# Forgetting attention in a two-layer decoder trunk: the gates' running sums added to the scores on VectorE from a table that is broadcast through memory, instead of by a product with a selection matrix

## The chip, the cores and the metric

The kernel runs on one core of one Trainium2 chip. The core has five instruction streams that run side by side and each in its own order: TensorE (PE in the profile, its weight loads are PEld), VectorE (DVE), ScalarE (ACT), GpSimd (POOL) and SyncE (SP), which here issues all DMA transfers. The metric is the device time of one execution in microseconds (us), as the median of several executions. The activations and the weights are float32; large products are made from float32 values that are split in a high and a low part.

## The reference, cut to what matters

The trunk has two layers over 256 tokens of 1024 values. Layer 0 mixes tokens with forgetting attention ("FoX", 16 heads of 64), layer 1 with latent attention. Each layer has two SwiGLU half-steps and an embedding gate around its mixer. Only the mixer of layer 0 is touched:

```
def fox_mixer(x, w_in, b_f, w_o):
    h = x @ w_in
    q = h[..., :D_MODEL].reshape(B, S, FOX_HEADS, FOX_HEAD_DIM)
    k = h[..., D_MODEL:2 * D_MODEL].reshape(B, S, FOX_HEADS, FOX_HEAD_DIM)
    v = h[..., 2 * D_MODEL:3 * D_MODEL].reshape(B, S, FOX_HEADS, FOX_HEAD_DIM)
    f_logit = h[..., 3 * D_MODEL:].astype(jnp.float32) + b_f.astype(jnp.float32)
    cum = jnp.cumsum(jax.nn.log_sigmoid(f_logit), axis=1).transpose(0, 2, 1)
    ...
        s = jnp.einsum('bqhd,bkhd->bhqk', qb, k).astype(jnp.float32) * scale
        return s + cb[:, :, :, None] - cum[:, :, None, :]
    ...
    o = causal_block_attention(scores, v)
    return o.reshape(B, S, D_MODEL) @ w_o
```

`qb` and `cb` are the queries and their running sums; the last call does the causal mask, the softmax and the product with v. `cum[h, t]` is the running sum of the log gates of head h up to token t. The term of the query is constant along a row of the scores; the term of the key, `-cum[h, s]`, differs from column to column and is what the change moves to another engine.

## The kernel before

**Precision.** A float32 operand is split in hi (ScalarE copies it to fp32r) and lo (VectorE subtracts hi); a product is hi·hi + hi·lo + lo·hi, three matmuls (`mm3`). Weights come from memory in `raw` tiles of 1 MB (three buffers), are split by L193/L194 (or L201/L205, the two halves apart) into `hl` slots and then used. `Stream` plans where in the program each split stands, by estimated clocks of PE, ACT and DVE that `busy()` advances; `load()` issues the next `raw` transfer on SP as soon as a group of weights is split, so SP waits there for the DVE instruction that frees the buffer.

**FoX, before the heads.** `fox()` first makes V (`VA`, `VB`, `VC`). `VC` also yields the 16 gate logits of each token. `gates()` transposes them (so that head h sits in partition 112+h, time along the free dimension) and puts the rest of the gate's work in small steps s1 to s6 into the queue `bg`, one of which is taken out at each `use` of a weight and at k = 3 and 6 inside `ws`. The steps compute log sigmoid (ACT Exp and Ln, some POOL arithmetic at L931 to L941, one DVE reciprocal), the running sum over time (a scan on DVE, L946, into `sc`), and `m8` = -8 times it (POOL, L947). Steps s4 to s6 lay `m8`, split in hi and lo, into `negc` [128, 384]: ACT L951 and L952, DVE L955, L958 and L962. `sel` [128, 16] is a constant 0/1 matrix that picks a head.

**The heads.** Eight rounds j = 0 to 7, two heads each (s = 0, 1, in partitions 0 to 63 and 64 to 127 of the `qk` tile). In round j PE makes k of the next pair (`gen_k(j+1)`, 24 matmuls), the transposes of the finished probabilities of the last pair (`T(j-1)`), the scores (`QK(j)`), q of the next pair (`gen_q(j+1)`, 24 matmuls) and the product with V (`AV(j-1)`). In round 7 the output projection `O` takes the place of the generators. `QK(j)` first fills each of the two score banks with one product of 64 contraction rows and 384 columns, the selection column of the head times `negc`, which puts -8·cum of every key in every row; the 12 matmuls of q·k are accumulated on top. Of the 384 columns, 0:128 are query block 0 against keys 0 to 127, and 128:384 are query block 1 against all 256 keys.

`softmax(j)` runs on DVE and ACT: L1028 adds the causal mask `self.mask` to the bank, scales it by -1/8 and takes the row minimum, four times; L1035 and L1036 do a small correction of that minimum with `cq`, the running sums by token (cum of the query drops out of the softmax); ACT L1040 takes the exponential, four times. `divide` is one DVE reciprocal and two POOL multiplications (L1050) for each head. `T(j)` in the next round needs what L1050 wrote.

**The tile `gb`** holds gain and bias of a layer norm (L543, L544: two broadcast transfers of 512 KB). In FoX it is loaded for the norm after the mixer, in round 2.

What sets the order around the change: each engine runs its list in order, so an instruction that waits holds up everything behind it on its engine; SP's list has the weight transfers and the small ones in one line.

## Time and profile before

| | us |
|---|---|
| median of three runs (lowest, highest) | 1077.59 (1077.35, 1078.14) |
| the profiled execution, whole | 1080.02 |
| its span in the profile | 1077.9 |
| busy in the span: PE, PEld | 1064.3, 974.0 |
| busy in the span: DVE, ACT, POOL | 721.5, 543.8, 60.2 |
| one matmul of `negc` with `sel` (16 of them, in eight pairs) | 0.44 |
| first and last pair start at | 222.0, 280.5 |

The profile shows one execution. All times below are microseconds from the start of its span. "Busy" of PE is modelled, since matmuls overlap: where one ends is less certain than where it starts, so distances between starts are the safer measure. A row of the timeline gives start, duration, engine, line, operation, tiles written and read, shapes and, in brackets, how long the engine sat idle before it and what ended that. A row with "x12" is twelve instructions in a line, and its duration runs from the first start to the last end. The rounds of FoX lie between 222 and 289 us.

### The profile page before, as it was taken

The page shows a single profiled execution, that of the slowest core. Times are in us where ns is not written, and L with a number is a line of the kernel's source. Part 1 is how long each engine was busy: PE and PEld are TensorE (multiplying, and loading weights), DVE is VectorE, ACT ScalarE, POOL GpSimd, SP SyncE. Part 2 cuts the span into 40 slices and gives each one's busy share as a digit, 9 for nine tenths or more (in the row PEclk, how much of TensorE's full clock was granted, in tenths as well). Part 3 has the DMA queues.
Part 4 walks back from the last instruction along what each step waited for, and adds up shares of the span by engine and source line. Part 5 has one row for each costly group of instructions (what it writes and reads, how often), then busy time and mean ns, then how long its engine had stood idle before and what let it go on. Part 6 is the DMA issues. An engine that isn't in the chain of part 4 may idle for free.

```text
span 1077.9 us, 17528 instructions
## 1 busy us (share of the span) xinstructions
PE 1064.3 (99%) x7236; PEld 974.0 (90%) x7236; DVE 721.5 (67%) x1053; ACT 543.8 (50%) x805; POOL 60.2 (6%) x94
## 2 busy tenths in 40 slices
PE   9999999999999999999999999999999999999997
PEld 8989998999889899998899999988889789898986
DVE  5675545788897545548966554389877886455566
ACT  5654433667655444444564443337666465344431
POOL 0000000223100000001320000010000000000000
PEclk9999999999999999999999999999999999999999
DMA  7885642543348655444477554334334568555502
GB/s 276 335 297 222 236 159 93 204 173 118 130 177 296 233 191 196 146 177 166 168 262 274 195 194 148 108 93 147 130 126 159 185 225 314 181 207 188 186 11 78
DMA packets 33092, 199.58 MB, mean 185 GB/s; under 512 B 3699, under 2 KB 5491, under 8 KB 12149
## 3 DMA queue, kind: packets, MB, share of 16 engines
q1 hardware_dynamic: 33012, 198.47, 51.5%
q8 instruction: 57, 0.93, 0.3%
q14 instruction: 23, 0.18, 0.1%
HBM read 197.40 MB, written 1.05 MB: 184 GB/s over the span
## 4 chain that ended last, share of the span: by engine, by line
PE 87%; DVE 8%; ACT 2%; issue 1%; POOL 1%; DMA 0%; DVEq 0%; SPq 0%; POOLq 0%; ACTq 0%
PE y L489 31%; PE h L489 31%; PE tr L489 22%; DVE hl L194 2%; PE tr L493 2%; ACT P L1425 1%; DVE x L569 1%; ACT hl L193 1%; DVE PT L499 1%; DVE tr L1420 0%; DVE st L551 0%; DVE x L550 0%; PE h L493 0%; DVE qk L499 0%; DVE hl L205 0%
## 5 line engine op out<-in xcount | busy, mean ns | idle before, releaser
L194 DVE TENSOR_TENSOR hl<-raw,hl 128x1024 fp32r<-128x1024 f32 (+3 forms) x267 | 312.8, 1191 | 149.5 <-ACT hl L193 148.3
L193 ACT ACTIVATE hl<-raw 128x1024 fp32r<-128x1024 f32 (+3 forms) x267 | 269.3, 1031 | 184.9 <-PE y L489 97.6
L489 PE MATMUL y<-hl,g 128*128 128x512 f32 x816 | 190.7, 390 | 0.0
L489 PE MATMUL h<-xT,hl 128*128 128x256 f32 x1560 | 188.0, 280 | 0.4 <-DVE hl L233 0.2
L489 PEld LDWEIGHTS h<-xT,hl 128*128 128x128 f32 x1560 | 183.4, 190 | 2.6 <-ACT xT L498 0.6
L489 PEld LDWEIGHTS y<-hl,g 128*128 128x128 f32 x816 | 152.0, 188 | 30.7
L489 PE MATMUL tr<-xT,hl 128*128 128x256 f32 x1512 | 176.6, 277 | 0.0
L489 PEld LDWEIGHTS tr<-xT,hl 128*128 128x128 f32 x1512 | 174.2, 188 | 0.5
L489 PE MATMUL h<-hl,xT 128*128 128x512 f32 (+2 forms) x300 | 67.8, 374 | 0.4 <-DVE xT L499 0.4
L489 PE MATMUL y<-hl,xT 128*128 128x512 f32 (+3 forms) x360 | 65.4, 334 | 0.0
L489 PEld LDWEIGHTS h<-hl,xT 128*128 128x128 f32 x300 | 53.2, 188 | 10.7 <-DVE xT L499 1.0
L489 PEld LDWEIGHTS y<-hl,xT 128*128 128x128 f32 x360 | 55.5, 188 | 6.3 <-ACT xT L498 0.4
L561 POOL TENSOR_TENSOR rs<-ve,mhalf 128x1 f32<-128x1 f32 x16 | 15.1, 943 | 633.7 <-DVE ve L560 633.7
L489 PE MATMUL y<-hl,otb 128*128 128x512 f32 x168 | 43.8, 402 | 1.2 <-DVE otb L499 1.0
L499 DVE TENSOR_TENSOR g<-P,g 128x512 fp32r<-128x512 f32 x38 | 26.3, 693 | 26.6 <-ACT g L498 26.6
L498 ACT ACTIVATE xT<-tr 128x512 fp32r<-128x512 f32 x28 | 16.1, 597 | 49.3 <-PE tr L493 49.3
L498 ACT ACTIVATE g<-P 128x512 fp32r<-128x512 f32 x38 | 24.1, 634 | 32.7 <-DVE P L678 32.7
L489 PEld LDWEIGHTS y<-hl,otb 128*128 128x128 f32 x168 | 30.6, 192 | 7.8 <-DVE otb L499 1.4
L194 DVE TENSOR_TENSOR otb<-raw,otb 128x1024 fp32r<-128x1024 f32 (+1 forms) x20 | 24.1, 1203 | 17.3 <-ACT otb L193 17.3
L194 DVE TENSOR_TENSOR qk<-raw,qk 128x1024 fp32r<-128x1024 f32 (+1 forms) x21 | 25.7, 1222 | 12.0 <-ACT qk L193 12.0
L677 ACT ACTIVATE P<-tr 128x512 f32<-128x512 f32 x20 | 12.0, 600 | 39.3 <-PE tr L489 39.3
L678 DVE TENSOR_TENSOR P<-P,tr 128x512 f32<-128x512 f32 x20 | 13.8, 688 | 25.0 <-PE tr L489 13.4
(264 smaller groups left out, 1411.1 us busy)
## 6 DMA issues: line engine op xcount, KB each, us to landing
raw<-in_ffn_in_dram SPq DMA_DIRECT2D x85, 1024.0 KB, 4.9
raw<-in_ffn_out_dram SPq DMA_DIRECT2D x44, 1024.0 KB, 5.0
raw<-in_pg_dram SPq DMA_DIRECT2D x8, 1024.0 KB, 4.8
raw<-in_mo_dram SPq DMA_DIRECT2D x8, 1024.0 KB, 4.7
raw<-in_kq_dram SPq DMA_DIRECT2D x8, 640.0 KB, 5.2
gb<-in_ln_g_dram SPq DMA_DIRECT2D x8, 512.0 KB, 5.8
gb<-in_ln_b_dram SPq DMA_DIRECT2D x8, 512.0 KB, 7.3
raw<-in_fk_dram SPq DMA_DIRECT2D x4, 1024.0 KB, 4.9
```

The source lines that it names most:

```text
L193: nc.scalar.activation(hi, src, AF.Copy)
L194: nc.vector.tensor_tensor(lo, src, hi.bitcast(F32), op=ALU.subtract)
L489: self.nc.tensor.matmul(out, lhsT, rhs, start=start, stop=stop)
L493: self.nc.tensor.transpose(out, in_, self.ident)
L498: self.nc.scalar.activation(hi, src, AF.Copy)
L499: self.nc.vector.tensor_tensor(lo, src, hi.bitcast(F32), op=ALU.subtract)
L561: nc.gpsimd.tensor_tensor(rs, ve, self.mhalf, op=ALU.pow)
L569: nc.vector.scalar_tensor_tensor(xs, xs, rs if i else mv[:, 0:1], self.gb[:, i, c0:c1], op0=ALU.mult if i else ALU.subtract, op1=ALU.add i ...
L677: nc.scalar.activation(gt, ps[0], AF.Silu)
L678: nc.vector.tensor_tensor(gt, gt, ps[1], op=ALU.mult)
L1425: nc.scalar.activation(P[:, c0:c1], b[:, c0:c1], AF.Exp, bias=nm[:, q : q + 1], scale=-1.0, accum_out=su[:, q : q + 1],)
```

## The change

The table of -8·cum now goes out to memory and comes back broadcast: step s4 stores the 16 rows of `m8` in a DRAM tile `fox_c` [16, 256]; `decay_load(j)` reads the two rows of round j back into all 128 partitions of a new tile `mb` [128, 2, 2, 384] (two buffers by j modulo 2, two heads, 384 columns), in two transfers, columns 0:128 and 128:384; `decay_mask(j)` writes the causal mask's -1e30 into it with two POOL instructions (L928), one for each diagonal block. `softmax` reads `mb` where it read `self.mask`, so the same DVE instruction now adds mask and decay. `sel`, `negc`, steps s5 and s6 and the product in `QK` go. In the gate's steps, two subtractions move from POOL to DVE and an idle step goes. `mb` takes the memory of `gb`; so the load of the layer norm's gain and bias moves from round 2 to the end of round 7's softmax.

```diff
-        sel = self.tl([128, 16], F32R, "sel", 1)
-        negc = self.tl([128, 384], F32R, "negc", 1)
+        mb = self.tl([128, 2, 2, 384], F32, "gb", 1)
...
+        def decay_load(j):
+            if not self.rec:
+                o = mb[:, j % 2]
+                for c0, n in ((0, 128), (128, 256)):
+                    row = self.fox_c[2 * j, 0:1]
+                    src = bass.AP(tensor=row.tensor, offset=row.offset, ap=[[0, 128], [256, 2], [1, n]])
+                    nc.sync.dma_start(o[:, :, c0 : c0 + n], src)
+        def decay_mask(j):
+            for c0 in (0, 256):
+                o = mb[:, j % 2, :, c0 : c0 + 128]
+                nc.gpsimd.affine_select(
+                    out=o, in_=o, pattern=[[0, 2], [-1, 128]], compare_op=ALU.is_ge, fill=NEG,
+                    base=0, channel_multiplier=1,
+                )
...
-                nc.gpsimd.tensor_tensor(e, r, e, op=ALU.subtract)
+                nc.vector.tensor_tensor(e, r, e, op=ALU.subtract)
...
-                nc.gpsimd.tensor_tensor(u, e, ab, op=ALU.subtract)
                 nc.gpsimd.memset(r, 0.0)
...
             def s3():
+                nc.vector.tensor_tensor(u, e, ab, op=ALU.subtract)
...
             def s4():
-                nc.scalar.activation(negc[fr, 0:128], m8[:, 0:128], AF.Copy)
-                nc.scalar.activation(negc[fr, 128:384], m8, AF.Copy)
-
-            def s5():
-                nc.vector.tensor_tensor(
-                    negc[64:96, 128:384], m8, negc[fr, 128:384].bitcast(F32), op=ALU.subtract
-                )
-                nc.vector.tensor_copy(negc[64:96, 0:128], negc[64:96, 128:256].bitcast(F32))
-                self.S.busy(dve=400)
-
-            def s6():
-                nc.vector.tensor_copy(negc[0:64, :], negc[64:128, :].bitcast(F32))
+                self.dma(self.fox_c, m8[16:32, :])
+                for j in range(2):
+                    decay_load(j)
+                    decay_mask(j)
-            self.bg.extend((s1, rest, rest, s2, rest, rest, s3, rest, s4, s5, s6))
+            self.bg.extend((s1, rest, rest, s2, rest, rest, s3, s4))
...
-            for s in range(2):
-                h = 2 * j + s
-                self.mm(
-                    sb[s][:, 0:384], sel[half[s], h : h + 1].to_broadcast([64, 128]), negc[half[s], :],
-                    True, False,
-                )
...
-                            o[half[s], jj, 256 : 256 + c1 - c0], False, n == 2 and q0 > 0,
+                            o[half[s], jj, 256 : 256 + c1 - c0], n == 0 and q0 == 0, n == 2 and q0 > 0,
...
-                        out=sb[s][:, c0:c1], in0=sb[s][:, c0:c1], in1=self.mask[:, c0:c1],
+                        out=sb[s][:, c0:c1], in0=sb[s][:, c0:c1], in1=mb[:, j % 2, s, c0:c1],
...
             divide(1)
+            if j < 6:
+                decay_load(j + 2)
+            if 1 <= j < 7:
+                decay_mask(j + 1)
+            if j == 7:
+                self.load_gb(li, 1)
...
-            if j == 2:
-                self.load_gb(li, 1)
```

Where this moves instructions: on PE eight pairs of matmuls go, on ACT the two copies to `negc`, and the rest of those two lists is unchanged, in all of the program. DVE, POOL and SP change as follows. (`fs` is the tile of the gate's intermediate values; `g` here holds V.)

On DVE, the gate's steps s2 to s4 and the parts of the first k and q, of before:

```order
L938 RECIPROCAL fs<-fs 32x256
L194 TENSOR_TENSOR hl_2153<-raw,hl_2153 128x1024
L499 TENSOR_TENSOR g_2156<-y,g_2156 128x512
L945 SCALAR_TENSOR_TENSOR fs<-fs 32x256
L946 SCALAR_TENSOR_TENSOR fs<-fs 32x256
L499 TENSOR_TENSOR qk<-h,qk 128x256
L194 TENSOR_TENSOR hl_2193<-raw,hl_2193 128x1024
L955 TENSOR_TENSOR negc<-fs,negc 32x256
L958 CAST negc<-negc 32x128
L962 CAST negc<-negc 64x384
L499 TENSOR_TENSOR qk<-h,qk 128x256
```

and of the change:

```order
L950 RECIPROCAL fs<-fs 32x256
L194 TENSOR_TENSOR hl_2150<-raw,hl_2150 128x1024
L499 TENSOR_TENSOR g_2153<-y,g_2153 128x512
L956 TENSOR_TENSOR fs<-fs 32x256
L957 SCALAR_TENSOR_TENSOR fs<-fs 32x256
L958 SCALAR_TENSOR_TENSOR fs<-fs 32x256
L499 TENSOR_TENSOR qk<-h,qk 128x256
L194 TENSOR_TENSOR hl_2208<-raw,hl_2208 128x1024
L499 TENSOR_TENSOR qk<-h,qk 128x256
```

One subtraction (L956) now stands ahead of the scan and of the first `qk` part; the three instructions on `negc` are gone. The other moved subtraction stands four rows ahead of the RECIPROCAL, in front of an `hl` split.

On SP, from the last `fk` weights to the output weights, of the change (before, the rows of `fox_c` were not there and the two rows of `gb<-in_ln` stood behind the first `fo`):

```order
L367 DMA raw<-in_fk_dram 128x2048
L419 DMA fox_c<-fs 16x256
L922 DMA gb<-fox_c 128x2x128
L922 DMA gb<-fox_c 128x2x256
L922 DMA gb<-fox_c 128x2x128
L922 DMA gb<-fox_c 128x2x256
L367 DMA raw<-in_fq_dram 128x2048
L922 DMA gb<-fox_c 128x2x128
L922 DMA gb<-fox_c 128x2x256
L367 DMA raw<-in_fo_dram 128x2048
```

The store, the four reads of rounds 0 and 1, and their waits stand ahead of the last `fq` weights; after that a pair of reads stands ahead of each of the next six weight transfers.

On POOL, from the last gate step to the divisions of rounds 0 to 2, of the change:

```order
L959 TENSOR_SCALAR fs<-fs 32x256
L928 AFFINE_SELECT gb<-gb 128x2x128 x4
L1048 TENSOR_SCALAR P<-P,su 128x128
L1048 TENSOR_SCALAR P<-P,su 128x256
L1048 TENSOR_SCALAR P<-P,su 128x128
L1048 TENSOR_SCALAR P<-P,su 128x256
```

The masks of rounds 0 and 1 stand ahead of the first division; from round 1 on the two masks of the next round stand behind the four divisions of a round. Before, nothing stood between the gate step and the divisions.

More of the change, by code (lines that the diff above doesn't have):

```diff
@@ L397, with __init__ @@
 class Trunk:
-    def __init__(self, nc, pools, a, S, rec):
-        self.nc, self.a, self.S = nc, a, S
+    def __init__(self, nc, pools, a, S, rec, fox_c=None):
+        self.nc, self.a, self.S, self.fox_c = nc, a, S, fox_c
         self.sb, self.ps = pools
@@ L909, in fox @@
         nc.gpsimd.memset(fs, 0.0)
-        nc.gpsimd.memset(negc.bitcast(F32), 0.0)
-        sf = fs[:, 1792:1808]
-        nc.gpsimd.tensor_tensor(sf, self.ident[:, 16:32], self.ident[:, 48:64], op=ALU.add)
-        nc.gpsimd.tensor_tensor(sf, sf, self.ident[:, 80:96], op=ALU.add)
-        nc.gpsimd.tensor_tensor(sel, sf, self.ident[:, 112:128], op=ALU.add)
         f, e, u, r, ab = (fs[fr, 256 * i : 256 * i + 256] for i in range(5))
@@ L1535, in tile_trunk @@
     ps = ctx.enter_context(tc.tile_pool(name="ps", bufs=1, space=bass.MemoryType.PSUM))
+    dr = ctx.enter_context(tc.tile_pool(name="dr", bufs=1, space=bass.MemoryType.DRAM))
     ctx.enter_context(tc.manual_schedule())
@@ L1543, in tile_trunk @@
     S = Stream(nc, raw, sb, make_loads(a), r.seq)
-    Trunk(nc, (sb, ps), a, S, False).run()
+    Trunk(nc, (sb, ps), a, S, False, dr.tile([16, 256], F32, name="fox_c")).run()
 _INS = ["x", "p", "ln_g", "ln_b", "ple_b_gate", "fox_b_f", "mla_q_norm", "kv_norm"]
```

## The prediction

> **What bounds the kernel now.** I read the page first: the busy times, then the chain of waits.
>
> ```profile
> PE 1064.3 (99%) x7236; PEld 974.0 (90%) x7236; DVE 721.5 (67%) x1053; ACT 543.8 (50%) x805; POOL 60.2 (6%) x94
> PE 87%; DVE 8%; ACT 2%; issue 1%; POOL 1%; DMA 0%; DVEq 0%; SPq 0%; POOLq 0%; ACTq 0%
> ```
>
> PE is busy nearly all the time and carries 87% of the chain that ended last. So what leaves PE's list is gained, unless PE then waits. Next the view by stretches, for one round of FoX (length; then busy us of PE, PEld, DVE, ACT, POOL; clock; DMA share, GB/s):
>
> ```profile
> 237.90:246.40 8.50, 8.50 (x75) 8.09 (x74) 7.22 (x23) 6.01 (x17) 2.56 (x4) 1.00 0.34 126
> ```
>
> PE has no pause in the round, DVE 1.3 us of 8.5, POOL 5.9, and DMA uses a third of its time. Last the timeline around the second product, which shows what a product costs.
>
> ```profile
> 223.01 5.73 PE L489 MATMUL h<-xT,hl 128*128 128x256 f32 x48
> 228.49 0.46 PEld L1065 LDWEIGHTS tr<-ident,P 128*128 128x128 f32 x4
> 229.33 0.19 PEld L489 LDWEIGHTS y<-negc,sel 64*128 64x128 f32 x2 [0.17 <-issue]
> 229.33 0.45 PE L489 MATMUL y<-negc,sel 64*128 64x384 f32 x2
> 229.44 0.83 PEld L489 LDWEIGHTS y<-qk 64*128 64x128 f32 x12
> 229.62 0.85 PE L489 MATMUL y<-qk 64*128 64x128 f32 x12
> 230.40 3.01 PE L489 MATMUL h<-xT,hl 128*128 128x256 f32 x24
> ```
>
> The two matmuls of a pair start together: their two heads lie in different halves of the rows and run side by side. So eight pairs count, not sixteen matmuls.
>
> **The product that goes.** From its start to the first q·k matmul is 229.62 - 229.33 = 0.29 us, the upper bound of a round's gain. But the 0.29 holds a weight load that nothing covers: load and matmul are noted at one start, and the next load follows 229.44 - 229.33 = 0.11 later. Without the product the first load of q·k stands uncovered there instead. 0.29 - 0.11 = 0.18 is left. The columns say the same: 48 matmuls of 256 columns take 228.59 - 223.01 = 5.58 us (the transposes' first matmul starts 0.10 behind the load at 228.49), or 0.116 each, and 384 columns 0.174. Lower bound 0.11, one load's distance, should loads alone set the pace. I take 8 x 0.18 = 1.45 us (0.9 to 2.3). The 0.17 of "issue" ahead of the group stays, since the change from 128 to 64 rows stays.
>
> **The gate's chain ahead of round 0.**
>
> ```profile
> 215.25 1.80 POOL L940 TENSOR_TENSOR fs<-fs 32x256 f32<-32x256 f32 x1
> 216.36 0.68 DVE L499 TENSOR_TENSOR g<-y,g 128x512 fp32r<-128x512 f32 x1
> 217.08 0.42 DVE L945 SCALAR_TENSOR_TENSOR fs<-fs 32x256 f32<-32x256 f32 x1
> 217.60 0.69 DVE L946 TENSOR_TENSOR_SCAN fs<-fs 32x256 f32<-32x256 f32 x1
> 218.32 0.42 DVE L499 TENSOR_TENSOR qk<-h,qk 128x256 fp32r<-128x256 f32 x1
> 218.38 0.41 POOL L947 TENSOR_SCALAR fs<-fs 32x256 f32<-32x256 f32 x1 [1.08 <-DVE fs L946]
> 218.80 2.81 PEld L489 LDWEIGHTS h<-xT,hl 128*128 128x128 f32 x24 [0.34 <-DVE qk L499]
> 219.91 0.42 DVE L955 TENSOR_TENSOR negc<-fs,negc 32x256 fp32r<-32x256 f32 x1
> ```
>
> The subtraction L940 ends on POOL at 217.05, as DVE ends its part of V at 217.04: it is hidden. On DVE it stands between 217.04 and L945 and costs what L955, of the same form, takes: 0.42. The scan and the `qk` part behind it move by that. PE already waits 0.34 for this part, since the part frees the bank for k of the next pair; it waits 0.42 longer. The other moved subtraction, another 0.42 on DVE, falls where DVE waited for ACT, and may push a split a little: bounds 0.3 and 0.6, I take 0.5 lost. What the change frees on ACT and DVE (copies to `negc`) lies behind this wait and shortens nothing that PE waits for.
>
> **The round trip through memory.** `m8` is ready at 218.79 before and at 219.3 now. There it went to `negc`; now the store leaves then, its landing releases the reads, theirs the masks, and these the DVE pass of round 0, behind which DVE's in-order list holds `qk` parts and a split, and for which ACT's exponentials, the divisions and T(0) wait. The store's queue is free: the `fk` weights were issued at 212.60 and take 4.9.
>
> ```profile
> 212.60 0.33 SPq L367 DMA_DIRECT2D raw<-in_fk_dram  x1
> raw<-in_fk_dram SPq DMA_DIRECT2D x4, 1024.0 KB, 4.9
> bf<-in_fox_b_f_dram SPq DMA_DIRECT2D x1, 0.1 KB, 1.5
> out_dram<-x SPq DMA_DIRECT2D x3, 256.0 KB, 2.0
> raw<-in_w_dram SPq DMA_DIRECT2D x2, 128.0 KB, 2.4
> gb<-in_ln_g_dram SPq DMA_DIRECT2D x1, 512.0 KB, 3.5
> gb<-in_ln_b_dram SPq DMA_DIRECT2D x1, 512.0 KB, 5.9
> 229.47 0.43 SPq L419 DMA_DIRECT2D gb<-in_ln_g_dram  x1
> ```
>
> The store is 16 KB. The nearest rows are the smallest transfer, 1.5, and the stores of the output, 2.0; I take 1.9, so 221.2. The first read (128 KB) leaves then, the second (256 KB) 0.43 later. For a read: 2.4 for 128 KB on a nearly idle queue, 3.5 for a broadcast of 512 KB on an idle one (the last two transfers are from the stretch 500 to 510). I take 2.45 from the second issue: 224.1. (Upper bound: as `ln_b`, which was queued right behind `ln_g`.)
>
> ```profile
> L454 POOL TENSOR_SCALAR_AFFINE_SELECT mask<-mask 128x128 f32<-128x128 f32 x2 | 0.5, 294 | 1.2 <-PE y L465 1.2
> L1050 POOL TENSOR_SCALAR P<-P,su 128x256 f32<-128x256 f32 x16 | 7.7, 481 | 0.0
> 223.51 0.43 DVE L1028 CUSTOM_DVE_ANT_0 y<-y,mask 128x256 f32<-128x256 f32 x1
> 226.88 0.83 POOL L1050 TENSOR_SCALAR P<-P,su 128x128 f32<-128x128 f32 x2 [0.21 <-DVE su L1047]
> ```
>
> A mask covers 256 elements of a partition: between 0.29 (128 elements) and 0.48 (256, another operation); 0.45. So the 256-column pass of DVE starts at 224.55 in place of 223.51, 1.04 late, and the last division ends at 226.88 + 0.83 + 1.04 = 228.75. T(0) came at 228.49 and now comes at 228.49 + 0.5 - 0.18 = 228.81. The delay just fits: 0 lost, with the upper bound 3.4 worked out below. The masks of round 1 stand ahead of round 0's divisions on POOL, but those reads leave 0.43 apart too; they end before 226.86, when the first division is due.
>
> [...]
>
> **Rounds 1 to 7.** Each adds two reads and two masks.
>
> ```profile
> 233.41 0.83 POOL L1050 TENSOR_SCALAR P<-P,su 128x128 f32<-128x128 f32 x2 [5.70 <-DVE su L1047]
> 234.37 1.20 DVE L205 TENSOR_TENSOR hl<-raw,hl 128x1024 fp32r<-128x1024 f32 x1
> 234.54 1.72 POOL L1050 TENSOR_SCALAR P<-P,su 128x128 f32<-128x128 f32 x2 [0.30 <-DVE su L1047]
> 236.70 1.23 DVE L205 TENSOR_TENSOR fs<-raw,fs 128x1024 fp32r<-128x1024 f32 x1
> 237.03 0.46 PEld L1065 LDWEIGHTS tr<-ident,P 128*128 128x128 f32 x4
> 239.40 0.29 DVE L1028 CUSTOM_DVE_ANT_0 y<-y,mask 128x128 f32<-128x128 f32 x1
> ```
>
> The reads have a whole round (8.5 us) to land. The masks of round 2 start at 236.26, when the divisions of round 1 end, and are due at 239.40. A division beside a DVE split takes 0.9 longer (1.72 against 0.83 for two): the split at 234.37 holds POOL up. So one mask may wait for the split at 236.70 to end at 237.93, and is done by 238.4: 1.0 to spare. T(1) follows its divisions by 237.03 - 236.26 = 0.77; a round that is 0.18 shorter leaves 0.59. Cost 0; if a mask holds the split up, at most 0.5 of delay, still inside 0.59.
>
> [...]
>
> **SP and the tail.** The last `fq` weights leave at 222.9, behind the reads, in place of 219.90, and land by 227.8. The splits at 234.37 and 236.70 are still the two of the `fk` group of 212.60, so the `fq` group is read after 237.9: 10 us to spare. The norm's gain and bias now leave behind round 7's pass and are read 16 us later:
>
> ```profile
> 219.90 0.33 SPq L367 DMA_DIRECT2D raw<-in_fq_dram  x1
> 284.38 0.17 DVE L1047 RECIPROCAL su<-su 128x2 f32<-128x2 f32 x1
> 300.40 0.74 DVE L569 SCALAR_TENSOR_TENSOR x<-x,mv,gb 128x512 f32<-128x512 f32 x1
> ```
>
> Even 5.9 each, one after the other, ends before. Cost 0; without that cover the norm, and PE behind it, would start later by what is missing.
>
> **The sum.** -1.45 + 0.5 + 0 = -0.95 us. The profiled execution took 1080.02 (2.1 outside its span), so 1079.07 there; on the median of the runs, 1077.59 - 0.95 = **1076.6**. By the terms' own bounds (0.9 to 2.3, 0.3 to 0.6, 0 to 0.5) this case reaches from 1075.6 to 1077.8.
>
> **The rivals.**
>
> 1. *The round trip decides T(0), and the kernel gets slower.* If the first read takes 3.5 and the second lands as `ln_b` did, 5.9 after its issue, it is there at 221.63 + 5.9 = 227.5; the pass starts at 228.05, 4.5 late, T(0) 3.4 late. PE's list stands still as long: -0.95 + 3.4 = +2.45, 1080.0. It costs from a landing at 224.1 on, us for us, and turns the sign from 225.05 on. For it: reads of 512-byte and 1-KB pieces of the same 2 KB, which no row shows, and `ln_b` itself. Against: an idle queue, and less data.
> 2. *The gain in full.* The uncovered load vanishes too and the gates' delay is at its least: -2.3 + 0.3 = -2.0, or -2.3 with none, 1075.3 to 1075.6. For it: the 0.29 as noted. Against: every change of row count in the rows shows the load uncovered.
> 3. *The masks come late in every round.* Two as long as the slowest POOL instruction above, 1.80, end at 239.86, 0.64 past their due time in a round 0.18 shorter; past the 0.59 of room that is 0.05 in each of six rounds, 0.3: 1076.9.
> 4. *Little is gained:* weight loads set the pace, -0.9 + 0.5 = -0.4, 1077.2.
>
> **The numbers.** Forecast 0.42, rival 1 0.30, rival 2 0.12, rival 3 0.06, rival 4 0.10. 0.2% is 2.16 us, about what a measurement of this kernel can tell from no change. Faster than that needs all of rival 2: with a little of the forecast 0.11. Slower needs rival 1 beyond a landing at 227.2, or worse than its price: its price lies past that, so of its 0.30 some 0.24 do, with 0.01 from elsewhere. Within: 0.64. The range, 1075.3 to 1080.0, goes from rival 2 to rival 1's price; the forecast's own is the one above.
>
> **What would show it.** In the changed profile: the distance from the last transpose to the first matmul behind q·k 0.18 shorter in each round; PE's wait for the `qk` part 0.8 in place of 0.34; the store at 219.3 and the second read landed near 224.1; T(0) without a wait for POOL; no PE wait in rounds 1 to 7; the same splits and loads behind 290. It is wrong if PE waits for T(0) by more than 0.5, if the rounds keep their 8.5 us, or if a later stage differs.

## The result: slower by 0.3%

The changed kernel takes 1081.31 us (median of 13 runs, 1079.11 to 1083.56), the kernel before beside it 1077.84 (13 runs, 1076.76 to 1079.74). The ratio is 1.0031, with a 95% interval of 1.0024 to 1.0039: 2.6 to 4.2 us more. The forecast was 1076.6, its range ended at 1080.0. The profiled execution of the changed kernel took 1083.13, its span 1081.6.

From its page, the busy times and the granted clock in 40 slices, and from the view of waits what PE waited for between 205 and 295:

```profile
PE 1064.4 (98%) x7220; PEld 973.0 (90%) x7220; DVE 720.9 (67%) x1052; ACT 542.0 (50%) x803; POOL 61.4 (6%) x104
PEclk9999999989999999999999999999999999999999
PE tr L1069 <- POOL P L1048: 1.2, 1, 1.2
PE h L489 <- DVE qk L499: 0.8, 1, 0.8
```

The busy times differ by less than 2 us and don't show where the loss lies. The 8 in the clock row is in the slice that holds the first rounds of FoX, and there PE waits for POOL ahead of T(0), which it did not before (there, T(0) starts 0.13 behind the last matmul ahead of it, at 228.59).

**The measure used below.** Starts of PE's instructions are the safer measure, so FoX is cut at them: G is the first transpose of the gate logits (204.44 before, 204.20 in the changed kernel), Q(j) the first matmul of `QK(j)`, T(7) the last pair's first transpose. Worked out from the timelines of all profiles, in us:

```
                    G..Q(0)  Q(0)..Q(1)  Q(1)..Q(2)  Q(2)..Q(7)  Q(7)..T(7)   G..T(7)   against before
before               17.52      7.37        8.55       42.59        7.75       83.78
changed kernel       18.00     10.05       11.12       42.02        7.53       88.72      +4.94
```

So 0.5 is lost ahead of round 0, 5.3 in two rounds, and 0.8 is gained in all the others. Behind FoX, some 1.5 comes back that the change did not earn: the profiled execution of before has a stretch of half clock at 790, shown further down, and this one has not.

**The stretch of 5.3.** The timeline of the changed kernel from the gates to T(0) (start, duration, engine, line, operation, tiles):

```profile
217.84 0.69 DVE L958 TENSOR_TENSOR_SCAN fs<-fs 32x256 f32<-32x256 f32 x1
218.56 0.42 DVE L499 TENSOR_TENSOR qk<-h,qk 128x256 fp32r<-128x256 f32 x1
219.04 3.01 PE L489 MATMUL h<-xT,hl 128*128 128x256 f32 x24 [0.79 <-DVE qk L499]
219.05 0.33 SPq L419 DMA_DIRECT2D fox_c<-fs  x1
220.49 1.92 SPq L922 DMA_DIRECT2D gb<-fox_c  x4
223.09 5.92 PE L489 MATMUL h<-xT,hl 128*128 128x256 f32 x48
224.09 0.41 POOL L928 TENSOR_SCALAR_AFFINE_SELECT gb<-gb 128x256 f32<-128x256 f32 x1 [5.07 <-DMA gb<-fox_c]
226.12 0.41 POOL L928 TENSOR_SCALAR_AFFINE_SELECT gb<-gb 128x256 f32<-128x256 f32 x1 [1.61 <-DMA gb<-fox_c]
226.56 0.43 DVE L1026 CUSTOM_DVE_ANT_0 y<-y,gb 128x256 f32<-128x256 f32 x1 [1.66 <-POOL gb L928]
227.13 0.41 POOL L928 TENSOR_SCALAR_AFFINE_SELECT gb<-gb 128x256 f32<-128x256 f32 x1 [0.60 <-DMA gb<-fox_c]
228.64 0.16 DVE L1045 RECIPROCAL su<-su 128x2 f32<-128x2 f32 x1
229.34 0.41 POOL L928 TENSOR_SCALAR_AFFINE_SELECT gb<-gb 128x256 f32<-128x256 f32 x1 [1.81 <-DMA gb<-fox_c]
229.74 1.63 POOL L1048 TENSOR_SCALAR P<-P,su 128x128 f32<-128x128 f32 x4
230.16 1.73 PE L1069 MATMUL tr<-ident,P 128*128 128x128 f32 x4 [1.15 <-POOL P L1048]
```

Four masks of POOL wait for four reads, each starting as its read lands: 224.09 and 226.12 for round 0, 227.13 and 229.34 for round 1. The second read, issued some 0.43 behind the first, thus lands 5.1 us after its issue, where the forecast took 2.45; the 256-column pass of DVE, at 223.51 before, starts at 226.56, 3.05 late. (The reads were not alone: the last `fq` weights, 1 MB, left right behind them at 222.51. What that adds to their landing, no run parts.) The divisors of head 0 are there at 228.80, but POOL's list has both masks of round 1 first, and the last one waits for its read until 229.34: the divisions begin at 229.74. T(0) starts 1.3 us later behind PE's work than before, and its transposes then follow the divisions: the four and the next one take 231.69 - 230.16 = 1.5 in place of 0.4. Together a stall of 2.4 us.

The view by stretches of the changed kernel then shows what comes behind it (length; busy us of PE, PEld, DVE, ACT, POOL with counts; granted clock; DMA share, GB/s):

```profile
228.01:231.42 3.41, 1.99 (x12) 1.21 (x11) 1.81 (x8) 2.89 (x10) 2.02 (x5) 1.00 0.68 255
231.42:238.25 6.83, 6.83 (x35) 6.28 (x36) 5.28 (x19) 3.64 (x11) 1.23 (x3) 0.50 0.55 198
238.25:241.66 3.41, 3.41 (x28) 3.27 (x27) 1.89 (x4) 2.01 (x4) 2.03 (x4) 1.00 0.23 80
```

A stretch of 3.41 us in which PE is busy for 1.99 is followed by 6.83 us at half clock (the 0.50 in the second row), in which the 256-column matmuls start 0.213 apart instead of 0.118. That costs about half of 6.83, and the sum of the two rounds agrees: 2.68 + 2.57 = 5.25 lost, plus the 0.2 to 0.35 that two products less give, minus the stall of 2.4, leaves about 3.1. **More is lost behind the stall than in it.**

### The profile page after: what moved, and what is told of

Read it like the earlier page. It is cut to its first block, busy times and chain, and to the rows that moved or that the text cites. A ratio compares the mean times of both kernels' runs of the same rounds, so it can differ in the third digit from the quotient of the medians.

```text
span 1081.6 us, 17560 instructions
## 1 busy us (share of the span) xinstructions
PE 1064.4 (98%) x7220; PEld 973.0 (90%) x7220; DVE 720.9 (67%) x1052; ACT 542.0 (50%) x803; POOL 61.4 (6%) x104
## 3 DMA queue, kind: packets, MB, share of 16 engines
HBM read 200.55 MB, written 1.06 MB: 186 GB/s over the span
## 4 chain that ended last, share of the span: by engine, by line
PE 62%; DVE 8%; ACT 2%; issue 1%; POOL 0%; DVEq 0%; POOLq 0%; ACTq 0%
PE y L489 24%; PE h L489 20%; PE tr L489 17%; DVE hl L194 2%; PE tr L493 1%; ACT P L1427 1%; DVE x L569 1%; DVE PT L499 0%; DVE tr L1422 0%; DVE st L551 0%; DVE x L550 0%; ACT hl L193 0%; DVE hl L205 0%; PE h L493 0%; DVE qk L499 0%
```

## The experiments

Two theories stood against each other at first: that the late reads alone make the loss, or that something in every round does. The answer came out as three mechanisms, and the runs are told by them. "us" is the median against the kernel before on the same chip; the cuts of FoX stand in one table at the end.

### The late reads, the order of masks, the gates, the product

`e1_mask_order` puts the masks of round 1 behind the divisions of round 0.

```diff
                 for j in range(2):
                     decay_load(j)
-                    decay_mask(j)
+                decay_mask(0)
...
-            if 1 <= j < 7:
+            if j < 7:
                 decay_mask(j + 1)
```

> The masks of round 1 move on GpSimd from ahead of round 0's divisions to behind them; nothing else. Theory 'late landing' (the table's reads land late, and both the scores' passes and the mask of round 1 that waits for the fourth read hold T(0)): head 0 can be divided from 228.8 instead of 229.7 and head 1 from 229.9 instead of 230.5, since su is there by 228.80 and 229.88; T(0) comes 0.6 to 0.9 us earlier, TensorE is still late by some 2.1 us, and the second read still lands some 5 us behind its issue; 1080.4 to 1080.9 if the half clock behind the stall stays, about 1077 if the shorter stall doesn't bring it on. Rival 'GpSimd's order alone' (the mask of round 1 is the whole cause): T(0) isn't waited for at all, 1076.9. Rival 'steady cost' (something in every round): no change, 1081.3.

1081.74 against 1078.52, ratio 1.0028 (1.0017 to 1.0040). By the starts around T(0) the stall fell from 2.4 to 1.8 us, and this execution had no half clock (Q(0) to Q(2) lost 1.7 against before, not 5.3). Yet the median over nine executions is hardly better than that of the changed kernel; their mean granted clock, 0.9973 against 0.9979 before, suggests that the half clock came in others. So POOL's order is a part, and the landing is the larger part.

`e2_early_read` takes rows of `x` instead of the stored sums and reads them early.

```diff
-                    row = self.fox_c[2 * j, 0:1]
+                    row = a["x"][0, j, 0:1]
...
-                for j in range(2):
-                    decay_load(j)
-                    decay_mask(j)
...
         VC(0, {4: lambda: self.XT(1, (0,)), 7: lambda: self.XT(1, (1,))})
+        for j in range(2):
+            decay_load(j)
+            decay_mask(j)
         VB(0)
```

> The reads take rows of the input x, which is in memory from the start, in place of the stored sums (so what is added to the scores is not the decay), and the reads and masks of rounds 0 and 1 are issued ahead of VB(0), some 15 us before they are used; the store stays, unread. Theory 'late landing': no wait of TensorE for T(0), no half clock behind it, the 0.8 us wait for the qk part stays; 8 x 0.18 saved less 0.45 lost at the gates: 1.0 below the kernel before, 1076.8, and 4.5 below the changed kernel. Rival 'steady cost': still 1080 to 1081. Rival 'the selection product was hidden': 0.45 above before, 1078.3.

1078.87 against 1078.52, ratio 0.9998 (0.9985 to 1.0010). No wait for T(0), no half clock in FoX: the loss of the changed kernel in the first rounds is the late landing, with what hangs on it. The expected gain of 1.0 did not come: FoX takes as long as before. Of that, the wait for the `qk` part took 1.2 where 0.8 was expected; the rest is what the third group is about.

`e3_no_product` takes the two matmuls of `sel` and `negc` out of the kernel before and starts the banks with q·k.

> The kernel before with the two selection products of each round left out (the decay isn't added to the scores); the table of sums is still computed. Price of the product alone. Theory 'the product lies on TensorE's path at 0.18 us a round': 1.45 below before, 1076.4 (ratio 0.9987). Rival 'it was hidden': no change, 1077.8. If TensorE is as full as it seems and a gap opens elsewhere instead, between the two.

1077.81 against 1078.52, ratio 0.9987 (0.9975 to 0.9999); FoX is 1.1 shorter. A round is 8.37 in place of 8.54, the 0.17 of the forecast, but two of the eight gain nothing (Q(0) to Q(1) keeps 7.4, and the last interval 8.4).

`e4_gates_pool` puts the two subtractions of the gates back on POOL in the changed kernel.

```diff
-                nc.vector.tensor_tensor(e, r, e, op=ALU.subtract)
+                nc.gpsimd.tensor_tensor(e, r, e, op=ALU.subtract)
...
+                nc.gpsimd.tensor_tensor(u, e, ab, op=ALU.subtract)
...
-                nc.vector.tensor_tensor(u, e, ab, op=ALU.subtract)
```

> The changed kernel with the two subtractions of the gates back on GpSimd; nothing else. Theory 'late landing': the sums are there 0.45 us sooner, TensorE waits 0.34 us again for the qk part instead of 0.79, the stall before T(0) keeps its length: 0.45 below the changed kernel, 1080.9, still with the half clock. Rival 'the gates on VectorE are the main cause': 3 or more below, 1078 or less.

1081.08 against 1078.52, ratio 1.0029 (1.0015 to 1.0044). PE's wait for the `qk` part is 0.32 again, G to Q(0) is 17.62 in place of 18.00: the term is 0.4, and it is not the main cause. The half clock is there again.

### The half clock

`e5_fill` gives PE spare transposes while it waits at T(0).

```diff
+            def warm(n):
+                for _ in range(n):
+                    self.transpose(b1[:, 0:128], self.ident)
+            if j == 0:
+                warm(11)
...
+                    if j == 0 and s + q < 2:
+                        warm(3)
```

> The changed kernel with spare transposes of the identity ahead of and between those of T(0): 11 ahead of the first, 3 behind each of the first two (1.9 us of work whose result is overwritten), in the time in which TensorE waits there. The wait itself stays. Theory 'a stall halves the clock' (the granted clock drops for one or two stretches of 3.41 us behind a stretch that is largely idle): no half clock at 231 to 238, and 1.7 to 3.4 us below the changed kernel where the drop is there in most executions: 1078 to 1079.6. Rival 'the half clock comes from elsewhere (the reads, the masks)': it stays, 1081.3 or a little more.

1081.16 against 1078.31, ratio 1.0027 (1.0018 to 1.0035). In the profile the half clock is gone (the granted clock is 1.00 from 228.85 to 235.68) and Q(1) to Q(2) is 8.36 in place of 11.12; but Q(0) to Q(1) grew from 10.05 to 10.79, since the divisions of round 0 now fell beside a DVE split (2.60 for the four, in place of 1.63). So the forecast of 1078 to 1079.6 was missed: the median is hardly below that of the changed kernel, though the half clock is gone. What the half clock costs over all executions can be estimated from the mean granted clock, which each execution gives to three digits: 0.9968 over the changed kernel's 13 executions, 0.9980 here, 0.9979 in the kernel before. 0.0011 of 1080 us is 1.2 us a run, against 3.1 in the one that was profiled: it does not come at this length in every execution.

`e7_stall8` is the kernel before with a stall and no table: eight multiplications by one on POOL ahead of round 0's divisions; `e7_stall5` has five.

```diff
+            if j == 0:
+                for _ in range(8):
+                    nc.gpsimd.tensor_scalar(
+                        P[0][:, 128:384], P[0][:, 128:384], 1.0, 1.0, op0=ALU.mult, op1=ALU.mult
+                    )
             divide(0)
```

> The kernel before with eight multiplications by one on GpSimd ahead of round 0's divisions (8 x 0.49 = 3.9 us), so that they start where the changed kernel starts them; no table in it. Theory 'a stall halves the clock': T(0) comes 2.3 to 2.9 us late, and in most executions 1.7 to 3.4 us are lost at half clock behind it, as in the changed kernel: 1080.2 at the least, 1082 to 1083.5 with the half clock. Rival 'the half clock comes with the table (its reads or masks)': the stall alone, 1080.3, no half clock before the end in the profile.

> The kernel before with five multiplications by one ahead of round 0's divisions (2.45 us) in place of eight. Theory 'a stall halves the clock, if it fills enough of a stretch of 3.41 us': T(0) waits 0.1 to 0.5, its last transposes 1.2 in all, no half clock at 230 to 240; 1079.3. Rival 'any stall brings it on': half clock for 3.41 us or more, 1081 or more.

Eight: 1083.80 against 1078.31, ratio 1.0049 (1.0037 to 1.0062), mean clock 0.9955; FoX is 6.2 longer. Five: 1079.60 against 1077.85, ratio 1.0016 (1.0007 to 1.0026); FoX is 1.9 longer, with no half clock in it. So a stall alone brings the half clock, in a kernel that has neither table nor reads, and the shorter one that was profiled did not. In these profiles the clock changes at fixed steps of 3.41 us (before: at 790.75, 794.17 and 1074.06, which is 83 steps after 790.75; the changed kernel: at 231.42, 238.25 and 1077.92, 248 steps after 231.42), and the views by stretches show how long PE was busy in the step ahead of a change. Of `e7_stall8`, the step ahead of the change and the two behind:

```profile
229.65:233.06 3.41, 1.20 (x5) 0.63 (x6) 0.72 (x2) 0.38 (x1) 2.98 (x7) 1.00 0.55 183
233.06:239.89 6.83, 6.83 (x38) 6.28 (x37) 4.21 (x17) 3.65 (x11) 1.43 (x3) 0.50 0.53 217
```

Of `e4_gates_pool`:

```profile
230.87:234.28 3.41, 1.98 (x14) 1.25 (x16) 1.90 (x4) 2.98 (x9) 2.04 (x5) 1.00 0.43 152
234.28:237.70 3.42, 3.42 (x21) 3.20 (x20) 3.15 (x15) 2.01 (x6) 0.00 (x0) 0.50 0.74 234
```

Of the kernel before, in a place far from the change, where PE waits 1.4 us:

```profile
787.34:790.75 3.41, 2.00 (x17) 1.69 (x16) 3.38 (x7) 3.41 (x7) 0.00 (x0) 1.00 0.00 0
790.75:794.17 3.42, 3.42 (x14) 3.18 (x15) 2.65 (x5) 1.42 (x3) 0.00 (x0) 0.50 0.82 283
```

Of `e1_mask_order`, whose stall is cut in two by the step at 231.11 (247 steps ahead of its clock's change at 1074.19), the first part and the second:

```profile
227.70:231.11 3.41, 2.50 (x19) 1.92 (x17) 2.22 (x13) 2.52 (x10) 1.24 (x4) 1.00 0.68 266
231.11:234.52 3.41, 3.25 (x29) 2.77 (x30) 2.88 (x7) 2.63 (x5) 2.14 (x3) 1.00 0.57 139
```

Steps with PE busy for 1.20, 1.98, 1.99 and 2.00 us are followed by half clock; a step with 2.50 is not. The wait near 790 in the other traces narrows this: behind 2.01 (`e7_stall5`, the step at 788.41) half clock followed, behind 2.04 (`e3_no_product`, 786.80) and 2.05 (the changed kernel, 791.20) it did not. Away from the last 15 us of the program, no step of the traces of before and of the changed kernel with 2.05 or more was followed by half clock. Close below, it is not settled: 1.97 (`e2_early_read`, 787.74) and 2.00 (`e7_stall8`, 792.85) were not followed by it either. So in these traces the border lies near 2.0 of 3.41 us. Where the steps fall differs from profile to profile (one begins at 231.42 in the changed kernel, at 231.11 in `e1_mask_order`, at 230.87 in `e4_gates_pool`), so a stall can lie in one step, as in the changed kernel, or be shared by two, as in `e1_mask_order`.

### Faster reads, and a kernel without the stall

`e6_one_read` reads both heads' rows in one piece of 2 KB to each partition, and the first mask takes its columns out of it.

```diff
-                for c0, n in ((0, 128), (128, 256)):
-                    src = bass.AP(tensor=row.tensor, offset=row.offset, ap=[[0, 128], [256, 2], [1, n]])
-                    nc.sync.dma_start(o[:, :, c0 : c0 + n], src)
+                src = bass.AP(tensor=row.tensor, offset=row.offset, ap=[[0, 128], [1, 512]])
+                nc.sync.dma_start(mb[:, j % 2, 256:768], src)
...
```

> The changed kernel with one read a round in place of two: 2 KB in a row to each partition (128 pieces of 2 KB, 262 KB) instead of 512 B and 1 KB twice (512 pieces, 393 KB); the mask of the first block takes it out of that one read. Order of masks and gates as in the changed kernel. Theory 'the reads are slow by their number of pieces': the read of round 0 lands some 2.5 us behind its issue, that of round 1 at 3 to 3.5, T(0) is late by less than 1 us, no half clock, 1078.0. Rival 'slow by their bytes': it lands at 3.5 us and 5, T(0) is 1.5 to 2 us late, 1079.5 to 1080. Rival 'the landing is not what sets it': 1081.3.

1079.93 against 1078.31, ratio 1.0008 (0.9998 to 1.0018). The list of transfers shows the changed kernel's two kinds of reads (KB, median us from issue to landing) and, in the second fence, the one kind of `e6_one_read`:

```profile
gb<-fox_c SPq DMA_DIRECT2D x8, 256.0 KB, 4.4
gb<-fox_c SPq DMA_DIRECT2D x8, 128.0 KB, 3.5
```

```profile
gb<-fox_c SPq DMA_DIRECT2D x8, 256.0 KB, 3.5
```

The whole of round 0's table is there 3.5 us behind the issue, as early as the first of the two reads was; the 2.5 that was expected from fewer pieces did not come. T(0) doesn't wait for POOL, and there is no half clock in FoX. 128 KB in 256 pieces of 512 B and 256 KB in 128 pieces of 2 KB land equally soon (3.5 in the median), so neither bytes nor pieces alone set the time; the runs do not part the two further.

`e8_best` is e1, e4 and e6 together.

> The changed kernel with e1's order of the masks, e6's one read a round and e4's gates on GpSimd together. Theory 'late landing': the read of round 0 lands 2.5 to 3.5 us behind its issue, the first pass of VectorE is 0.5 to 1.5 us late, T(0) at most 0.5; no half clock; the product's price, measured at 0.7 to 1.0, is gained: 1077.0 to 1077.8, ratio to before 0.9988 to 0.9998. Rival (some cost of the table that is still unknown): 1079 or more.

1078.94 against 1078.31, ratio 1.0003 (0.9994 to 1.0011). Every wait that the change had brought to PE ahead of and in the first round is gone, and still next to nothing is gained: its rounds 2 to 6 take 42.76, against 42.59 before and 41.83 in e3.

### VectorE's round

The DVE timeline of a steady round tells why. Of `e3_no_product`, from one reciprocal of head 1 to the next (rows between are left out here and below):

```profile
260.28 0.17 DVE L1041 RECIPROCAL su<-su 128x2 f32<-128x2 f32 x1 [0.89 <-ACT P L1034]
262.71 1.23 DVE L205 TENSOR_TENSOR hl<-raw,hl 128x1024 fp32r<-128x1024 f32 x1
265.44 0.14 DVE L1022 DVE_READ_ACCUMULATOR2_ANT nm<- 128x1 f32 x1
265.62 0.43 DVE L1022 CUSTOM_DVE_ANT_0 y<-y,mask 128x256 f32<-128x256 f32 x1
268.67 0.17 DVE L1041 RECIPROCAL su<-su 128x2 f32<-128x2 f32 x1 [0.90 <-ACT P L1034]
```

Of `e8_best`, with POOL's masks:

```profile
262.39 0.17 DVE L1045 RECIPROCAL su<-su 128x2 f32<-128x2 f32 x1 [0.91 <-ACT P L1038]
264.32 0.76 POOL L927 TENSOR_SCALAR_AFFINE_SELECT gb<-gb 128x256 f32<-128x256 f32 x2
264.80 1.36 DVE L205 TENSOR_TENSOR hl<-raw,hl 128x1024 fp32r<-128x1024 f32 x1
267.67 0.14 DVE L1025 DVE_READ_ACCUMULATOR2_ANT nm<- 128x1 f32 x1
267.94 0.43 DVE L1025 CUSTOM_DVE_ANT_0 y<-y,gb 128x256 f32<-128x256 f32 x1
270.98 0.17 DVE L1045 RECIPROCAL su<-su 128x2 f32<-128x2 f32 x1 [0.91 <-ACT P L1038]
```

In both, DVE works through its list without a pause but one, 0.9 for ACT's exponentials, which themselves wait for DVE: the round is a closed loop of DVE and ACT. Without table it is 268.67 - 260.28 = 8.39 (8.38 over four rounds), with the table 270.98 - 262.39 = 8.59 (8.60 over four). The difference is the split, 1.36 in place of 1.23, and the second pass, which starts 0.27 behind the read of the first's minimum in place of 0.18. The kernel before has a PE round of 8.54. So PE can take out its product, but DVE's round with the table is longer than PE's was. In the changed kernel that was covered: while PE stood still and then ran at half clock, DVE came to be ahead of it, and the later rounds, 8.37 to 8.47 on PE against 8.60 on DVE, ate into that: T(2) starts 0.60 behind the end of its divisions, T(6) 0.16 ahead of it (the last division's).

`e9_mask_late` is e8 with the masks of rounds 2 to 7 in the time of the passes.

```diff
+            if 1 <= j < 7:
+                nc.gpsimd.tensor_scalar(bf, nm[:, 0:1], 1.0, 1.0, op0=ALU.mult, op1=ALU.mult)
+                decay_mask(j + 1)
             divide(0)
...
-            if j < 7:
-                decay_mask(j + 1)
+            if j == 0:
+                decay_mask(1)
```

> e8 with the masks of rounds 2 to 7 taken from behind the divisions, where they run beside VectorE's weight split, and put into the round's passes (a one-column copy of nm on GpSimd holds them until the first pass is done). Theory 'VectorE's loop' (in e8 VectorE runs without a pause but one of 0.90 us, and its round is 8.60 us with the table against 8.37 in e3 without it: 0.14 in the split beside the masks, 1.36 against 1.23, and 0.09 ahead of the second pass): the split is 1.23 again, the round 8.37 to 8.46, five rounds 0.7 to 1.1 us shorter than e8: 1077.9 to 1078.2, ratio to before 0.9992 to 0.9997. Rival 'the reads slow the round': it stays at 8.60, 1078.9.

1078.42 against 1077.85, ratio 1.0003 (0.9994 to 1.0012): a miss. The split is 1.22 again, but the masks now hold up the small instructions between the passes (a correction `tt` takes 0.35 in place of 0.16), the wait ahead of the second pass stays, and the loop is 8.65.

`e10_masks_only` adds work of the masks' size to e3, with no table and no reads.

```diff
+            if j < 7:
+                for c0 in (0, 128):
+                    o = self.mask[:, c0 : c0 + 256]
+                    nc.gpsimd.tensor_scalar(o, o, 1.0, 1.0, op0=ALU.mult, op1=ALU.mult)
```

> e3 (the kernel before without the product) with two multiplications by one on GpSimd behind each round's divisions, of the masks' size (128x256), on the mask that the passes read: the masks' work without table or reads. Theory 'VectorE's loop': the split of the round grows from 1.23 to 1.36 beside them and the round from 8.37 to 8.50 or 8.60: 0.6 to 1.3 us above e3, 1077.8 to 1078.4, as long as before. Rival 'the reads slow the round': 8.37 as in e3, 1077.1, ratio 0.9987.

1076.52 against 1077.85, ratio 0.9985 (0.9976 to 0.9994). The expected loss did not come; the loop is 8.48, not 8.60, and PE's rounds stay at 8.35, below it. They live on a lead of DVE: T(j) starts 0.93 behind the end of its divisions in round 0, 0.51 in round 2 and 0.06 in round 6. So the loop of this run never came to set the round. The timeline of `e10_masks_only` shows the split unharmed and POOL held up (1.95 for two, where a division of the same shape takes 0.48):

```profile
269.52 1.95 POOL L1053 TENSOR_SCALAR mask<-mask 128x256 f32<-128x256 f32 x2
269.99 1.23 DVE L205 TENSOR_TENSOR hl<-raw,hl 128x1024 fp32r<-128x1024 f32 x1
```

The second multiplication was due 0.02 behind the split's start. What is left of the 0.22 is the 0.10 ahead of the second pass. It appears where two instructions of POOL feed the two passes (0.26 to 0.28 behind the read of the minimum in e8, e9, e10 and e12) and not in e11, below, where one does (0.17); why is open.

`e11_mask_add` is e8 with the masks of rounds 1 to 7 made by one addition of the triangle.

```diff
...
+            if j > 0:
+                tri = self.mask[:, 0:128].unsqueeze(1).unsqueeze(1).to_broadcast([128, 2, 2, 128])
+                nc.gpsimd.tensor_tensor(o4, i4, tri, op=ALU.add)
+                return
...
```

> e8 with the masks of rounds 1 to 7 made by one addition of the triangle on GpSimd over all four blocks (128x512) in place of two selections; round 0 keeps its two selections. Theory 'VectorE's loop' (the selections hold up VectorE, in its split or in its passes: 8.60 and 8.65 us in e8 and e9; multiplications of GpSimd in e10 were held up themselves: 8.48): the loop of VectorE falls to 8.38 to 8.48, below the 8.54 of the kernel before, and the six rounds behind the first take 0.4 to 1.0 less than in the kernel before: 1077.0 to 1077.6, ratio 0.9992 to 0.9998, about where e3 and e10 stand but for the wait at the gates. Rival 'the reads slow the loop': it stays at 8.60, 1078.4, ratio 1.0003.

1082.34 against 1078.88, ratio 1.0032 (1.0023 to 1.0041): as slow as the changed kernel, with no stall of T(0) and no half clock in the FoX of its profile. The timeline of `e11_mask_add`:

```profile
266.18 1.28 POOL L928 TENSOR_TENSOR gb<-gb,mask 128x512 f32<-128x512 f32 x1
266.65 1.89 DVE L205 TENSOR_TENSOR hl<-raw,hl 128x1024 fp32r<-128x1024 f32 x1
```

The addition starts first, and the split ends 0.66 later than alone. The loop is 9.03, and PE's round too. The forecast, a loop of 8.38 to 8.48, was a miss, and the run shows the loop as the bound more plainly than any other run: 0.43 more in DVE's loop is 0.43 more in each round of the kernel.

`e12_masks_behind` leaves e8's masks as they are and only delays them on POOL, until the split has started.

```diff
+            if 1 <= j < 7:
+                for _ in range(2):
+                    nc.gpsimd.memset(mb[:, :, 768:1024], 0.0)
             if j < 7:
                 decay_mask(j + 1)
```

> e8 with two fills of an unused part of the tile (128x512 each, about 0.5 us) on GpSimd between a round's divisions and its masks, in rounds 1 to 6, so that the selections start behind VectorE's weight split and not 0.1 to 0.5 us ahead of it. Theory 'who starts first holds the other up' (e8: second selection at 264.68, split at 264.80, split 1.36; e10: split at 269.99, second multiplication at 270.01, split 1.23 and multiplication 1.47; e11: addition at 266.18, split at 266.65, split 1.89): the split is 1.23 again, a selection takes 1.2 or more, VectorE's loop is 8.46 to 8.48 as in e10, and the round is TensorE's 8.36; the kernel is 0.8 to 1.5 below the kernel before: 1076.4 to 1077.1, ratio 0.9986 to 0.9993. Rival 'the reads slow the loop': it stays at 8.60, ratio 1.0003.

1078.28 against 1078.47, ratio 0.9999 (0.9990 to 1.0009). The timeline of `e12_masks_behind`:

```profile
263.97 1.11 POOL L1058 MEMSET gb<- 128x512 f32 x2
264.46 1.23 DVE L205 TENSOR_TENSOR hl<-raw,hl 128x1024 fp32r<-128x1024 f32 x1
265.04 1.28 POOL L927 TENSOR_SCALAR_AFFINE_SELECT gb<-gb 128x256 f32<-128x256 f32 x2
```

Reads and masks are those of e8; only who starts first has changed. The split is 1.23, the loop 8.46, and FoX 0.6 shorter than in e8. So the reads don't slow the loop: with them it is 8.46, in e10 without them 8.48. The fills, which only write, did not hold up the split (1.23 beside them), and the selections, behind it now, take 1.28 for two in place of 0.76. The whole kernel gained less than forecast and can't be told from the kernel before.

All cuts of FoX, with the loop of DVE and ACT in rounds 2 to 5 where no stall covers it:

```
                    G..Q(0)  Q(0)..Q(1)  Q(1)..Q(2)  Q(2)..Q(7)   G..T(7)  against before   DVE loop
before               17.52      7.37        8.55       42.59       83.78                    8.54 (PE's)
e1_mask_order        18.09      9.13        8.46       42.73       85.94      +2.16
e2_early_read        18.37      7.40        8.44       42.06       83.81      +0.03         8.61
e3_no_product        17.51      7.40        8.37       41.83       82.69      -1.09         8.38
e4_gates_pool        17.62      9.60        9.93       42.22       86.91      +3.13
e5_fill              18.00     10.79        8.36       42.16       86.85      +3.07
e6_one_read          17.98      7.57        8.35       42.71       84.14      +0.36
e7_stall8            17.51     10.70       11.44       42.60       90.00      +6.22
e7_stall5            17.61      9.14        8.54       42.60       85.64      +1.86
e8_best              17.52      7.37        8.36       42.76       83.54      -0.24         8.60
e9_mask_late         17.51      7.36        8.45       43.11       83.97      +0.19         8.65
e10_masks_only       17.61      7.19        8.34       41.84       82.56      -1.22         8.48
e11_mask_add         17.61      7.42        8.91       45.18       86.66      +2.88         9.03
e12_masks_behind     17.53      7.43        8.35       42.10       82.95      -0.83         8.46
```

No version with the table beats the kernel before by more than can be measured; e3 and e10 do, but they leave the decay out.

The cuts are a better measure here than the medians, for one more reason. The part of a run that lies outside the span hardly varies within a kernel, but it differs between kernels: in the mean 2.0 us for the kernel before and 1.6 for the changed kernel, e1 and e5, 1.7 and 1.8 for e6 and e2, but 2.2 for e4, e8, e9, e11 and e12. So by their medians these five look some 0.6 worse beside the changed kernel than by their spans. Why, no run shows.

## Why the prediction was wrong

- **The product.** Right in size: from the first matmul of `QK` to the first behind it is 0.89 in place of 1.06, so 0.17 a round where 0.18 was said. Wrong in the count: alone (e3) it gains 1.1 in FoX, not 1.45, because the first and the last of the intervals don't shorten. Why those don't, no run shows.
- **The gates.** Right: the wait for the `qk` part is 0.79 (0.8 was named), and e4 takes it back to 0.32.
- **The round trip** is the step that failed. The store was sooner than taken: the first read leaves at 220.49, not 221.2. But "2.45 from the second issue: 224.1" measured 5.1, 226.06. The row it came from is one transfer of 128 KB; the rows for broadcasts (3.5 and 5.9) had been set aside as an upper bound, and the later one was the near one: four reads were queued within 1.9 us, and 1 MB of weights right behind them. From this follows the second error, on the masks of round 1: "they end before 226.86" became 229.75, so that POOL's divisions stood behind a read they don't need. e1, e2 and e6 show both: each removes a part of the lateness, e2 all of it, and its part of the stall goes.
- **Rival 1** had the place, the sign and nearly the size of the stall (3.4 said, 2.4 measured), and 1080.0 as its price. With the measured stall in place of 3.4 its sum is 1079.0, inside the range. A term that no case held is the half clock behind a stall, 3.1 in the profiled execution and an estimated 1.2 on average; what else carried the median to 1081.3 is open in part, as the account below says. "PE's list stands still as long" was priced us for us; e7_stall8 shows a stall of 3 us cost 6.2.
- **Rounds 1 to 7, "cost 0".** Wrong, though the changed kernel itself hides it. The text had seen that a mask may hold up the split, and weighed that against the 0.59 us of room of T; it was to be weighed against DVE's loop, which has no room but 8.54 - 8.38 = 0.16. e8 shows 0.22 more, and e12 takes 0.14 of it back.
- **SP and the tail.** Right in cost, wrong in a time: the `fq` weights, issued at 222.51 behind the four reads, land at 231.82 and not by 227.8, and PE waits for nothing there. Behind T(7), apart from the half clock at 790, no part differs by more than some 0.3.

The account of the medians: FoX without half clock is 4.9 - 3.1 = 1.8 longer, half clock costs 1.2 a run on average, and the time outside the span is 0.4 shorter (1.6 against 2.0 in the mean of all runs, for a reason that no run shows): 2.6, the lower edge of the 2.6 to 4.2 measured. Of the middle, 3.3, some 0.7 stays unexplained, and perhaps more: the four executions of the changed kernel at a mean clock of 0.998, where hardly any half clock can be, took 1080.8 in the mean, 2.8 above the 1078.0 of the kernel before, and the cuts of the one profile with the time outside the span give 1.4 of that.

## What to carry to other kernels

Ahead of taking work from the busiest engine, work out the next engine's loop for one round from its own timeline: here VectorE with ScalarE stood at 8.38 of 8.54 us, so at most 0.16 a round was to be had, and the change added 0.22 to that loop. Price a new wait of TensorE at up to twice its length (2.4 cost 5.5 in one profiled execution here, 3.0 cost 6.2 in another) when it may leave TensorE busy for no more than about 2.0 us of a step of 3.41, as these two did (1.99 and 1.20). And for a transfer that others wait for, take the row of the same shape that lands latest as the likely one (here 5.9, where 2.45 was taken and 5.1 measured), and put nothing on an in-order engine that waits for a later transfer ahead of work that waits for none (here the divisions, whose first divisors were there at 228.80, began at 229.74, behind a mask that waited for its read).

## What was not expected of the hardware

- The clock: five steps of 3.41 us with TensorE busy for 1.20 to 2.01 us were followed by half clock for 3.41 or 6.83 us, two with 1.97 and 2.00 were not, nor were those with 2.04, 2.05 and 2.50. The wait of 1.4 us at 787 cost some 1.5 us more in the profiled execution of before than in that of the changed kernel, which has the same wait and no half clock there (TensorE busy for 2.00 and 2.05 of the step).
- Who starts first: a selection of POOL, 0.12 us ahead of a VectorE split, lengthens the split from 1.23 to 1.36 (e8), an addition 0.47 ahead to 1.89 (e11); a multiplication due 0.02 behind the split waits itself, 1.95 for two (e10), and selections behind it take 1.28 for two in place of 0.76 (e12).
- Reads that broadcast the same 2 KB to 128 partitions land 3.5 (e6) and 3.4 us (e8) behind their issue in the median, even at one piece a partition; four of the changed kernel's in a row at 3.5, 5.1, 5.6 and 7.3.
